# Mask first in the attention scores, last products by column halves, a last norm in pieces, and the reciprocal root on POOL

## The chip, the cores and the metric

The kernel runs on one core of a Trainium2 chip. The metric is the device time of one execution in microseconds (us); lower is better. The engines are TensorE (PE in the profile, its weight loads PEld), VectorE (DVE), ScalarE (ACT), GpSimd (POOL), and SyncE (SP), whose queue issues the weight DMAs.

## The reference

The kernel computes a small decoder trunk in float32: 256 tokens of width 1024, two layers, each a mixer and a channel mixer with a residual add around both, and a last norm.

```python
def rms_norm(x, g):
    y = x * lax.rsqrt(jnp.mean(x * x, axis=-1, keepdims=True) + 1e-6)
    return y * g

for i in range(2):
    h = rms_norm(x, attn_norm[i])
    if i == 0:
        x = x + even_mixer(h, ...)     # heads A: 8 of 64, one shared key, top-64 of indexer scores
                                       # heads B: 8 of 64, causal; one output projection for both
    else:
        x = x + mla_mixer(h, ...)      # 16 heads, scores over 64 + 32 columns, causal
    h = rms_norm(x, ffn_norm[i])
    x = x + peer_ffn(h, ...)           # 8 heads, 16 of 16384 experts each, by product keys
return rms_norm(x, final_norm)
```

In each attention the scores of a 128-row block of queries get a mask (causal, or for heads A the keys that the indexer selected), then softmax, then the weighted sum of the values.

## The kernel before, in words

x stays in SBUF as four tiles x[tb][j] of 128 tokens by 512 columns: tb is the token block, j the column half. The stages run one after the other in the span: the even mixer (0 to 148 us), the first expert layer `peer` (149 to 947), the MLA mixer (948 to 1068), the second expert layer (1070 to 1868), the last norm.

Float32 products are made from a high half `hi` and a low half `lo` of each operand (fp32r), three matmuls for one product (hi by hi, lo by hi, hi by lo). The class `Weights` streams the weights: SP loads `raw`, ACT makes `hi` (L69), DVE makes `lo` (L70), and `split(j)` does that some four units ahead of the one that PE uses. The pools of `hi` and `lo` have five buffers, so a new split waits until PE has done with an older unit.

The last four units of a layer's final product go through `last4` (L82), which hands out products for token block 0, then 1; after a block, `add_to_x` (L459) adds both of its column halves to x on DVE (L463). The next layer begins with transposes of x on PE (`to_T`, L288). The tile framework schedules the recorded operations, so the rows of an engine can stand in another order than the code; the adds are recorded at a high priority.

`attention` (L347) treats four heads at a time. For each query block qb it takes two PSUM banks with two heads in each; for each head it issues QK (L372) and then a product of the identity `identb` with a bf16 mask (L374), which adds the mask to the scores in PSUM. DVE takes the row maxima (L379), ACT the exponential (L383), PE transposes P (L397, L399) and multiplies it with the values (L413, L414). The heads of a group are named by their first: B8 is the group of heads 8 to 11 in the even mixer, A4 that of heads 4 to 7. An operand of an even-numbered head lies in partitions 0 to 63, of an odd one in partitions 64 to 127 (even mixer); in MLA it fills 96. Attention steps are interleaved with the projections by a plan (PLAN0, PLAN1); the last two groups of the even mixer, A0 and B12, run after the input projections, with the output projection behind them.

`rsqrt` (L248) makes 1/sqrt(mean + eps) on DVE, by a shifted integer guess and three Newton steps on one column at a time. It serves `x_rstd` (L270; square sums on ACT, four calls over both token blocks and two in the last norm) and the two inner norms of MLA. `finish` (L810) is the last norm: the gain times x on POOL (L819), the factor on ACT (L822) and DVE (L823), four stores from SP (L825).

## Time and profile before

| | us |
|---|---|
| median of 3 runs | 1882.4 (1880.84 to 1884.98) |
| the profiled execution's own time | 1880.96 |
| its span on the core | 1879.2 |
| PE busy | 1852.2 (99%) |
| DVE busy | 1447.2 (77%) |
| ACT busy | 1247.3 (66%) |
| POOL busy | 6.4 |

A busy matmul counts from its start to a modelled end, so PE at 99% says that PE nearly always has an instruction at work, not that each runs at its peak. The rows further down show starts and durations; a start of one PE instruction taken from the start of the next gives its real pace.

### The profile page before, as it was taken

How to read it: one execution, taken by the hardware profiler on the slowest of the kernel's cores; microseconds unless marked ns; L12 is line 12 of the kernel's file. 1: busy time of each engine (PE TensorE's matmuls, PEld its weight loads, DVE VectorE, ACT ScalarE, POOL GpSimd, SP SyncE). 2: the span in 40 equal slices, each digit the busy share in tenths (PEclk: the TensorE clock that was granted, in tenths of full speed). 3: DMA queues.
4: the chain of work that ended last, by engine and by line, in shares of the span. 5: the costliest groups of instructions: out<-in, count | busy, mean ns of one | idle time of the engine just before them, and what ended most of it. 6: DMA issues, size and time to landing. Idle time of an engine off the chain costs nothing.

```text
span 1879.2 us, 35739 instructions
## 1 busy us (share of the span) xinstructions
PE 1852.2 (99%) x12588; PEld 1664.2 (89%) x12588; DVE 1447.2 (77%) x3710; ACT 1247.3 (66%) x3060; POOL 6.4 (0%) x10
## 2 busy tenths in 40 slices
PE   8999999999999999999999999999999999999997
PEld 7769999999999888888888799999999988888886
DVE  7958998888898666666677699988888976666665
ACT  5646556888887555555576665688888865555554
POOL 0000000000000000000000000000000000000001
PEclk9989999999999999999999999999999999999999
DMA  6415565555555555556554345655555555555554
GB/s 191 134 46 170 163 197 182 168 169 174 165 170 179 191 193 193 191 193 192 188 162 136 122 139 190 190 174 165 172 167 169 171 189 191 192 192 193 192 193 136
DMA packets 90179, 323.33 MB, mean 172 GB/s; under 512 B 10512, under 2 KB 10896, under 8 KB 89744
## 3 DMA queue, kind: packets, MB, share of 16 engines
q1 hardware_dynamic: 88704, 318.71, 52.6%
q8 instruction: 99, 1.62, 0.3%
q0 software_dynamic: 288, 2.10, 0.3%
q14 instruction: 80, 0.66, 0.1%
q10 hardware_dynamic: 1008, 0.25, 0.1%
HBM read 319.97 MB, written 1.05 MB: 171 GB/s over the span
## 4 chain that ended last, share of the span: by engine, by line
PE 92%; DVE 6%; ACT 1%; issue 1%; DMA 0%; ACTq 0%; DVEq 0%
PE S L806 13%; PE S L807 13%; PE S L808 13%; PE acc L1079 12%; PE acc L1080 12%; PE acc L1078 12%; PE scp L990 3%; PE pj L301 2%; PE pj L303 2%; PE pj L302 2%; DVE lo L70 2%; PE bk L372 1%; DVE A L834 1%; DVE A L831 1%; DVE A L838 1%; PE pj L438 1%
## 5 line engine op out<-in xcount | busy, mean ns | idle before, releaser
L69 ACT ACTIVATE hi<-raw 128x512 fp32r<-128x512 f32 (+2 forms) x1214 | 756.0, 628 | 566.6 <-DVE lo L70 198.0
L70 DVE TENSOR_TENSOR lo<-raw,hi 128x512 fp32r<-128x512 f32 (+2 forms) x1214 | 826.2, 685 | 351.4 <-ACT hi L69 344.8
L806 PE MATMUL S<-hi,hi 128*128 128x256 f32 x2048 | 579.3, 283 | 1.8 <-ACT A L1019 1.8
L808 PE MATMUL S<-hi,lo 128*128 128x256 f32 x2048 | 568.9, 278 | 0.4
L807 PE MATMUL S<-lo,hi 128*128 128x256 f32 x2048 | 568.7, 278 | 0.0
L806 PEld LDWEIGHTS S<-hi,hi 128*128 128x128 f32 x2048 | 386.0, 188 | 2.6 <-ACT A L1019 2.6
L808 PEld LDWEIGHTS S<-hi,lo 128*128 128x128 f32 x2048 | 384.7, 188 | 1.2 <-DVE lo L70 1.1
L807 PEld LDWEIGHTS S<-lo,hi 128*128 128x128 f32 x2048 | 385.4, 188 | 0.0
L1079 PE MATMUL acc<-lo,ohB 128*128 128x512 f32 x512 | 201.2, 393 | 0.0
L1079 PE MATMUL acc<-lo,ohA 128*128 128x512 f32 x512 | 201.2, 393 | 0.0
L1080 PE MATMUL acc<-hi,ohA 128*128 128x512 f32 x512 | 199.9, 391 | 0.0
L1080 PE MATMUL acc<-hi,ohB 128*128 128x512 f32 x512 | 199.2, 391 | 0.0
L1078 PE MATMUL acc<-hi,ohA 128*128 128x512 f32 x512 | 159.2, 390 | 0.0
L1078 PE MATMUL acc<-hi,ohB 128*128 128x512 f32 x512 | 159.2, 390 | 0.0
L955 ACT ACTIVATE ohB<-ohB,RA 128x128 bf16<-128x128 bf16 x256 | 117.2, 525 | 0.0
L1078 PEld LDWEIGHTS acc<-hi,ohA 128*128 128x128 f32 x512 | 96.1, 188 | 22.0
L1078 PEld LDWEIGHTS acc<-hi,ohB 128*128 128x128 f32 x512 | 96.1, 188 | 21.9
L1079 PEld LDWEIGHTS acc<-lo,ohA 128*128 128x128 f32 x512 | 96.2, 188 | 20.8
L1079 PEld LDWEIGHTS acc<-lo,ohB 128*128 128x128 f32 x512 | 96.2, 188 | 20.7
L1080 PEld LDWEIGHTS acc<-hi,ohB 128*128 128x128 f32 x512 | 96.2, 188 | 20.3
L1080 PEld LDWEIGHTS acc<-hi,ohA 128*128 128x128 f32 x512 | 96.2, 188 | 20.3
L957 ACT ACTIVATE ohB<-iota,RA 128x128 bf16<-128x128 f32 x256 | 84.1, 435 | 0.0
(263 smaller groups left out, 2465.8 us busy)
## 6 DMA issues: line engine op xcount, KB each, us to landing
raw<-in_pu SPq DMA_DIRECT2D x256, 512.0 KB, 3.6
raw<-in_pv SPq DMA_DIRECT2D x256, 512.0 KB, 4.3
raw<-in_pq SPq DMA_DIRECT2D x32, 512.0 KB, 3.6
raw<-in_w SPq DMA_DIRECT2D x20, 512.0 KB, 3.7
raw<-in_uq SPq DMA_DIRECT2D x9, 512.0 KB, 4.0
raw<-in_w SPq DMA_DIRECT2D x12, 352.0 KB, 2.9
raw<-in_w0o SPq DMA_DIRECT2D x8, 512.0 KB, 3.6
raw<-in_w1o SPq DMA_DIRECT2D x8, 512.0 KB, 3.9
```

The lines of the kernel that those rows point to most:

```text
L69: self.nc.scalar.activation(hi[:, :w], src, AF.Copy)
L70: self.nc.vector.tensor_tensor(lo[:, :w], src, hi[:, :w].bitcast(F32), op=OP.subtract)
L301: nc.tensor.matmul(ps[tb], hi[c][:, t], a, start=st, stop=False)
L806: nc.tensor.matmul(p, a, hi[c], start=first and i == 0, stop=False)
L807: nc.tensor.matmul(p, a, lo[c], start=False, stop=False)
L808: nc.tensor.matmul(p, b, hi[c], start=False, stop=last and i == 3)
L955: nc.scalar.activation(e[:, j // 2, :, j % 2], e[:, j // 2, :, j % 2], AF.Relu, bias=r[1], scale=r[2])
L957: nc.scalar.activation(e[:, j // 2, :, j % 2], iota, AF.Square, bias=r[0], scale=-1.0)
L990: nc.tensor.matmul(p[:, i], E[:, 1, i // 2, :, i % 2], G[:, s, i // 2, :, i % 2], start=i + s == 0, stop=True, skip_group_check=True)
L1078: nc.tensor.matmul(o, a[:, 0, t], w[0], start=b == 0, stop=False)
L1079: nc.tensor.matmul(o, a[:, 0, t], w[1], start=False, stop=False)
L1080: nc.tensor.matmul(o, a[:, 1, t], w[0], start=False, stop=b == NK - 1)
```

## The change

It has five parts. In `attention`, one mask product over both heads of a bank comes first (it starts the accumulation), and the four QK follow in the order of the heads, which alternate between the two banks. `last4` goes through the column halves outside and the token blocks inside, and after each of the four pieces yields, so that a piece of x is added at a time; the new splits are asked for as token block 1 has used a unit. `rsqrt` adds, scales and takes the power -0.5 on POOL, with a [128, 16] float32 constant `mhalf` (64 bytes in each partition). The last norm takes its square sums piece by piece behind the adds, multiplies one column half by the gain on POOL and the other on DVE together with the factor, and sends two of the four stores from ACT's queue.

```diff
     def last4(self, products):
-        j = self.pos
+        k = self.pos
         w = [self.next(self.look - i) for i in range(4)]
-        for tb in range(2):
-            for i in range(4):
-                products(i, w[i], tb)
-                if tb == 1:
-                    self.split(j + self.look + 1 + i)
-            yield tb
+        for j in range(2):
+            for tb in range(2):
+                for i in (j, j + 2):
+                    products(i, w[i], tb)
+                    if tb == 1:
+                        k += 1
+                        self.split(k + self.look)
+                yield tb, j
...
+        mhalf = cp.tile([128, 16], F32, name="mhalf")
+        nc.gpsimd.memset(mhalf, -0.5)
         def rsqrt(parts, n, name):
             k = parts[0].shape[1]
             v = small.tile([128, k], F32, name=name + "v")
-            nc.vector.tensor_scalar(v, parts[0], 1.0 / n, EPS, op0=OP.mult, op1=OP.add)
+            s = parts[0]
             for p in parts[1:]:
-                nc.vector.scalar_tensor_tensor(v, p, 1.0 / n, v, op0=OP.mult, op1=OP.add)
+                nc.gpsimd.tensor_tensor(v, s, p, op=OP.add)
+                s = v
+            nc.gpsimd.tensor_scalar(v, s, 1.0 / n, EPS, op0=OP.mult, op1=OP.add)
             y = small.tile([128, k], F32, name=name + "y")
-            t = small.tile([128, k], F32, name=name + "t")
-            nc.vector.tensor_single_scalar(t.bitcast(U32), v.bitcast(U32), 1, op=OP.logical_shift_right)
...
-            for c in (3.0, 12.0, 768.0):
...
-            nc.vector.tensor_scalar(y, y, -1.0 / 8192, None, op0=OP.mult)
+            nc.gpsimd.tensor_tensor(y, v, mhalf[:, :1].to_broadcast([128, k]), op=OP.pow)
             return y
...
-                for i in (0, 2, 1, 3):
-                    h = hs[i]
-                    o = v[i % 2][:, i // 2]
-                    l, r = qk(h, qb, nk)
-                    nc.tensor.matmul(o, l, r, start=True, stop=False, skip_group_check=True)
-                    mk, k0 = masks(h, qb)
-                    nc.tensor.matmul(o[:, k0:], identb, mk, start=False, stop=True, skip_group_check=True)
+                mk, k0 = masks(hs[0], qb)
+                for a in range(2):
+                    nc.tensor.matmul(v[a][:, :, k0:], identb, mk[:, None, :].to_broadcast([128, 2, nk - k0]),
+                                     start=True, stop=False, skip_group_check=True)
+                for i in range(4):
+                    l, r = qk(hs[i], qb, nk)
+                    nc.tensor.matmul(v[i % 2][:, i // 2], l, r, start=False, stop=True, skip_group_check=True)
...
+                    def part(tb, j):
...
+                        nc.scalar.activation(ps2.tile([128, 512], F32, name="S"), x[tb][j], AF.Square,
+                                             accum_out=ssq[:, tb, j:j + 1])
+                        if j == 0:
+                            nc.gpsimd.tensor_tensor(y[:, h[0]], x[tb][0], g[:, h[0]], op=OP.mult)
+                            return
+                        r = rsqrt([ssq[:, tb, 0:1], ssq[:, tb, 1:2]], D, f"fin{tb}")
+                        nc.scalar.activation(y[:, h[0]], y[:, h[0]], AF.Copy, scale=r)
+                        nc.vector.scalar_tensor_tensor(y[:, h[1]], x[tb][1], r, g[:, h[1]], op0=OP.mult, op1=OP.mult)
+                        for i in range(2):
+                            (nc.sync, nc.scalar)[1 - i].dma_start(out[tb * 128:(tb + 1) * 128, h[i]], y[:, h[i]])
...
-                for tb in W.last4(lambda i, w, tb: mm(NK - 2 + i // 2, ws[i // 2], w, tb, i % 2)):
-                    add_to_x(tb, lambda j: acc[tb][j])
-                if final:
-                    finish()
+                last = finish() if final else None
+                for tb, j in W.last4(lambda i, w, tb: mm(NK - 2 + i // 2, ws[i // 2], w, tb, i % 2)):
+                    add_to_x(tb, j, acc[tb][j])
+                    if final:
+                        last(tb, j)
```

The lines of the changed kernel are numbered a little differently: QK stays L372, its mask becomes L368, the adds become L460, the transposes L285, and `rsqrt` spans L254 to L265.

How PE's rows stand at group B8, first query block, before (`bk` are the two banks, `kbT` and `qbT` the keys and queries, `cnegb` the causal mask):

```order
L372 MATMUL bk_943<-kbT0_116,qbT0_114 128x128
L374 LDWEIGHTS identb_95
L374 MATMUL bk_943<-cnegb_96,identb_95 128x128
L372 MATMUL bk_943<-kbT0_116,qbT0_114 128x128
L374 LDWEIGHTS identb_95
L374 MATMUL bk_943<-cnegb_96,identb_95 128x128
L372 MATMUL bk_944<-kbT0_116,qbT0_114 128x128
L374 LDWEIGHTS identb_95
L374 MATMUL bk_944<-cnegb_96,identb_95 128x128
L372 MATMUL bk_944<-kbT0_116,qbT0_114 128x128
L374 LDWEIGHTS identb_95
```

And with the change:

```order
L368 LDWEIGHTS identb_95
L368 MATMUL bk_930<-cnegb_96,identb_95 128x256
L368 LDWEIGHTS identb_95
L368 MATMUL bk_931<-cnegb_96,identb_95 128x256
L372 MATMUL bk_930<-kbT0_118,qbT0_116 128x128
L372 MATMUL bk_931<-kbT0_118,qbT0_116 128x128
L372 MATMUL bk_930<-kbT0_118,qbT0_116 128x128
L372 MATMUL bk_931<-kbT0_118,qbT0_116 128x128
```

Two masks of 256 columns stand ahead of four QK that go from bank to bank; before, a mask of 128 columns stood behind each QK.

PE's rows at the start of the last two attention groups of the even mixer (group A0, first query block, with the selection mask `selm0`), before:

```order
L372 MATMUL bk_1245<-kkT_118,qaT_112 128x128
L374 LDWEIGHTS identb_95
L374 MATMUL bk_1245<-selm0_138,identb_95 128x128
L372 MATMUL bk_1245<-kkT_118,qaT_112 128x128
L374 LDWEIGHTS identb_95
L374 MATMUL bk_1245<-selm0_138,identb_95 128x128
L372 MATMUL bk_1246<-kkT_118,qaT_112 128x128
```

And with the change:

```order
L368 LDWEIGHTS identb_95
L368 MATMUL bk_1224<-selm0_140,identb_95 128x256
L372 MATMUL bk_1224<-kkT_120,qaT_114 128x128 x2
L368 LDWEIGHTS identb_95
L368 MATMUL bk_1225<-selm0_140,identb_95 128x256
L372 MATMUL bk_1225<-kkT_120,qaT_114 128x128 x2
L368 LDWEIGHTS identb_95
L368 MATMUL bk_1244<-cnegb_96,identb_95 128x256
L372 MATMUL bk_1244<-kbT1_119,qbT1_117 128x128 x2
```

Here the scheduler puts each bank's mask directly ahead of that bank's two QK ("x2" are two QK in a row), and the next bank's mask behind them.

DVE's rows at the end of the first expert layer (x00 and x01 are token block 0, x10 and x11 token block 1; `lo` are low halves of weights of MLA), before:

```order
L70 TENSOR_TENSOR lo_12191<-raw_12133,hi_12190 128x352
L463 TENSOR_TENSOR x00_73<-x00_73,acc_9004 128x512
L463 TENSOR_TENSOR x10_75<-x10_75,acc_9006 128x512
L70 TENSOR_TENSOR lo_12198<-raw_12133,hi_12197 128x352
L463 TENSOR_TENSOR x01_74<-x01_74,acc_9005 128x512
L463 TENSOR_TENSOR x11_76<-x11_76,acc_9007 128x512
L70 TENSOR_TENSOR lo_12207<-raw_12158,hi_12206 128x352
```

And with the change:

```order
L70 TENSOR_TENSOR lo_12131<-raw_12064,hi_12130 128x352
L460 TENSOR_TENSOR x00_73<-x00_73,acc_8960 128x512
L70 TENSOR_TENSOR lo_12140<-raw_12089,hi_12139 128x352
L460 TENSOR_TENSOR x10_75<-x10_75,acc_8962 128x512
L70 TENSOR_TENSOR lo_12155<-raw_12089,hi_12154 128x352
L460 TENSOR_TENSOR x01_74<-x01_74,acc_8961 128x512
L460 TENSOR_TENSOR x11_76<-x11_76,acc_8963 128x512
L70 TENSOR_TENSOR lo_12164<-raw_12114,hi_12163 128x352
```

A low half now stands between the first add and the second, and another between the second and the third; before there was one, in the middle.

## Rows read from the trace of the kernel before

Times in rows are us from the start of the span.

**Rows 1.** The page's parts 1 and 2: busy us of each engine (share of the span, instructions), and the clock that TensorE was granted in 40 slices of the span, 47 us each, in tenths of full speed.

```profile
PE 1852.2 (99%) x12588; PEld 1664.2 (89%) x12588; DVE 1447.2 (77%) x3710; ACT 1247.3 (66%) x3060; POOL 6.4 (0%) x10
...
PEclk9989999999999999999999999999999999999999
```

**Rows 2.** The waits of PE over the whole span: what it waited for, us in total, times, longest.

```profile
PE scp L288 <- DVE x L463: 3.6, 2, 1.9
```

**Rows 3.** The timeline of PE at group B8, the first attention group of the even mixer (start us, duration us, engine, line, operation, shapes, how many): first QK, first mask and second QK of the first query block, first QK of the second block, and the product behind them.

```profile
72.10 0.48 PE L372 MATMUL bk<-kbT,qbT 64*128 64x128 f32 x2
72.52 0.23 PE L374 MATMUL bk<-cnegb,identb 128*128 128x128 bf16 x1
...
74.41 0.70 PE L372 MATMUL bk<-kbT,qbT 64*128 64x256 f32 x2
...
77.44 0.48 PE L301 MATMUL pj<-hi,hi 128*128 128x512 f32 x1
```

**Rows 4.** The timeline of PE at the index scores (L572), 128 columns at 44 us and 256 columns at 56 us, with the product behind each.

```profile
44.11 0.71 PE L572 MATMUL bk<-kkT,iqT 64*128 64x128 f32 x8
44.75 0.50 PE L301 MATMUL pj<-hi,hi 128*128 128x512 f32 x1
...
56.32 1.13 PE L572 MATMUL bk<-kkT,iqT 64*128 64x256 f32 x8
57.38 0.50 PE L301 MATMUL pj<-hi,hi 128*128 128x512 f32 x1
```

**Rows 5.** The timeline of PE at group A4, second query block: the first QK and the instruction behind it, then the stretch from its first mask to the product behind it.

```profile
91.99 0.70 PE L372 MATMUL bk<-kkT,qaT 64*128 64x256 f32 x2
92.62 0.65 PE L413 MATMUL bk<-pT,vb 128*64 128x256 f32 x2
...
94.85 0.28 PE L374 MATMUL bk<-selm,identb 128*128 128x256 bf16 x1
95.06 0.70 PE L372 MATMUL bk<-kkT,qaT 64*128 64x256 f32 x2
...
96.68 0.48 PE L438 MATMUL pj<-hi,oT 128*128 128x512 f32 x1
```

**Rows 6.** Busy time by stretches, the sum over 70 to 100 us.

```profile
sum 30.00, PE 30.00 PEld 20.30 DVE 26.07 ACT 17.32 POOL 0.00; mean PE 10.00 PEld 6.77 DVE 8.69 ACT 5.77 POOL 0.00
```

**Rows 7.** The timeline of PE from the first QK of the last two attention groups of the even mixer: the first instruction, a QK of the second query block with its mask, the first transpose of P, the first product of the output projection.

```profile
107.36 0.49 PE L372 MATMUL bk<-kkT,qaT 64*128 64x128 f32 x2
...
112.87 1.22 PE L372 MATMUL bk<-kbT,qbT 64*128 64x256 f32 x2
114.03 0.29 PE L374 MATMUL bk<-cnegb,identb 128*128 128x128 bf16 x1
...
122.75 0.64 PE L397 MATMUL bk<-ident,P 128*128 128x128 f32 x2
...
131.43 0.50 PE L438 MATMUL pj<-hi,oT 128*128 128x512 f32 x1
```

**Rows 8.** Busy time by stretches, two of the last attention stretch (us of PE, PEld, DVE, ACT, POOL with their instructions, then granted TensorE clock, DMA share, GB/s).

```profile
114.00:117.00 3.00, 3.00 (x9) 1.33 (x8) 0.82 (x3) 1.60 (x6) 0.00 (x0) 0.50 0.00 0
126.00:129.00 3.00, 3.00 (x22) 2.08 (x21) 1.43 (x3) 1.12 (x3) 0.00 (x0) 0.98 0.00 0
```

**Rows 9.** The timeline of PE at the first attention group of MLA: a mask, the next QK and the QK after that.

```profile
1008.35 0.22 PE L374 MATMUL bk<-cnegb,identb 128*128 128x128 bf16 x1
1008.40 0.44 PE L372 MATMUL bk<-kT,qT 96*128 96x128 f32 x2
...
1008.74 0.44 PE L372 MATMUL bk<-kT,qT 96*128 96x128 f32 x2
```

**Rows 10.** The timeline of all engines at the end of the first expert layer: the last product, the adds to x (L463), the low half of a weight (L70) between them, the first transposes of MLA.

```profile
947.02 0.40 PE L1080 MATMUL acc<-hi,ohA 128*128 128x512 f32 x1
947.10 0.52 DVE L70 TENSOR_TENSOR lo<-raw,hi 128x352 fp32r<-128x352 f32 x1
...
947.53 1.28 DVE L463 TENSOR_TENSOR x<-x,acc 128x512 f32<-128x512 f32 x2
...
948.87 0.66 PE L288 MATMUL bk<-ident,x 128*128 128x128 f32 x4 [1.45 <-DVE x L463]
```

**Rows 11.** The timeline of ACT in the first expert layer: the last read of a square sum, and the scaled x.

```profile
161.37 0.18 ACT L275 ACTIVATION_READ_ACCUMULATOR S<-x 128x1 f32 x1
...
165.44 0.71 ACT L796 ACTIVATE xn<-x,xn2y 128x512 f32<-128x512 f32 x1
```

**Rows 12.** The timeline of POOL: the last of its four constants, and its multiplies in the last norm.

```profile
0.34 0.10 POOL L1150 MEMSET const-uint8-127<- 128x1 uint8 x1
...
1867.22 4.98 POOL L819 TENSOR_TENSOR raw<-x,raw 128x512 f32<-128x512 f32 x4 [798.13 <-DVE x L463]
```

**Rows 13.** The timeline of all engines at the end of the kernel: the last two products, the last read of a square sum, the last two operations of DVE.

```profile
1867.57 0.39 PE L1079 MATMUL acc<-lo,ohA 128*128 128x512 f32 x1
...
1867.80 0.40 PE L1080 MATMUL acc<-hi,ohA 128*128 128x512 f32 x1
...
1869.74 0.19 ACT L275 ACTIVATION_READ_ACCUMULATOR S<-x 128x1 f32 x1
...
1874.21 0.15 DVE L267 TENSOR_SCALAR xn1y<-xn1y 128x1 f32<-128x1 f32 x1
1874.47 0.49 DVE L823 TENSOR_SCALAR raw<-raw,xn1y 128x512 f32<-128x512 f32 x1
```

## What the change should do to the time

> **What bounds the kernel now.** I read the page's busy shares first: PE is busy 1852.2 of 1879.2 us, DVE 1447.2, ACT 1247.3, POOL almost not at all [rows 1]. A microsecond is gained where PE gets shorter work, or where PE stands still. The PEclk line shows one more thing: nine tenths or more of full clock in every slice but the third, 94 to 141 us, which has an 8. Next come PE's waits: it stands still at the three boundaries between layers, where the first transposes of the next layer wait for an add to x, 3.6 us in two of them [rows 2] and 1.5 us in one [rows 10]. After the last matmul, at 1867.80, another 11 us pass [rows 13]. So four places can pay: the attention scores, the clock's hole, the boundaries, the tail. The two expert layers hold nearly all of the matmuls, and their inner loops are as before.
>
> **Mask first: even mixer, groups B8 and A4.** PE's rows for B8 show each head as a QK of two instructions from 72.10 and its mask at 72.52; four heads of the first query block take 72.10 to 74.41, 2.31 us, and four of the second 74.41 to 77.44, 3.03 us [rows 3]. The change puts two wide masks ahead and lets the four QK alternate between banks, and since heads 0 and 1 lie in partitions 0 to 63 and 64 to 127, between halves of the array. What alternating QK cost, the index scores show, which have the same shape (64x128, 64x256) and alternate already: eight instructions, four heads' worth, take 44.11 to 44.75 = 0.64 us, and with 256 columns 56.32 to 57.38 = 1.06 us [rows 4]. A mask of 256 columns is some 0.21 us (94.85 to the QK at 95.06, the instruction behind it on PE) [rows 5]. So the first block becomes 0.64 + 2 x 0.21 = 1.06, a gain of 1.25; the second 1.06 + 0.42 = 1.48, a gain of 1.55.
>
> That alternation is worth 0.42 to 0.16 us per head has a rule beside it. The Trainium skill, "TensorE: Matmul & The Clock Gate", Part 3, The mechanism, says that a weight load passes matmuls in flight only if its row group differs. By it the alternating blocks gain as above and blocks whose neighbouring QK share a row group gain nothing on the QK; by a sum that gave every block the index scores' price, the last stretch below would gain some 6 us at full clock and not 0.75. The rows agree with the rule as far as they go.
>
> For A4 the order has mask, QK, mask, QK, QK, QK in the first block. Four heads of 0.58 now (the pitch of rows 3) are 2.3; afterwards I count 2 x 0.21 for masks, 0.42 for each QK that stands against a mask and 0.16 for the rest, 1.6: gain 0.7. The second block is now 0.63 + 0.63 for two early QK (91.99 to 92.62 is one) and 1.83 from 94.85 to 96.68 [rows 5], 3.1 together; two masks of 512 columns (0.23 each, the pitch of a product of 512 columns, as at 1867.57 and 1867.80 [rows 13]) and 1.06 make 1.5: gain 1.55. It now needs its selection mask before its first QK; that mask is written some 4 us before PE comes to it, so no wait follows. Together PE loses 5.05 us of work. DVE, however, is busy 26.07 of the 30 us from 70 to 100 [rows 6], so it can give up only 3.9 us before it is the bound. I take **-4** (bounds -1.5, if the two engines alternate less well, and -5).
>
> **Mask first: the last two groups, 107.36 to 131.43.** The output projection at 131.43 ends a stretch in which PE has attention alone. At 107.36 a head takes 0.58; from 112.87 a head's 256-column QK takes 1.16, and the transposes of P begin at 122.75 [rows 7]. The granted clock is 0.50 from 114 to 117 and back at 0.98 from 126 to 129 [rows 8], that is, the engine falls to 1.2 GHz after some 5 us in which it had 64-row QK and masks alone, and has 2.4 GHz back some 3 us after the transposes begin. In the new order a bank gets mask, QK, QK here, both QK from the same half, so they keep 0.42 (0.69 with 256 columns), and only every second mask goes: eight of 0.1 to 0.16 us, less what the kept ones grow, about 0.75 us at full clock. If the fall comes as long after the stretch's start as now, what is saved ahead of it pulls other work to full clock, and what is saved behind it counts double: together **-1.5**. From above, +1: the clock could fall earlier. From below, -7: kept at 2.4 GHz, the 13 us until 126 shrink by some 6.
>
> **Mask first: MLA.** A head is 0.34 us (1008.40 to 1008.74), of which the mask is 0.05 (1008.35 to 1008.40) [rows 9]; QK of 96 rows fill both halves and gain nothing by alternating, and a mask over two heads streams the same columns. Sixteen heads twice: **-0.5** (0 to -1.6, all of the pitch).
>
> **Column halves at the boundaries.** One expects DVE to have a single add left when PE stops. Between the first expert layer and MLA it now does: lo at 947.10, two adds from 947.53, transposes at 948.87, 1.85 us after the last product's start at 947.02 [rows 10]. But the transposes' wait, in both programs, is for the count of the last of the four adds, so no transpose starts sooner on its own column. And of the four weight halves of the last step, the second one is now released six products before the end, not earlier, which puts its successor's split (ACT hi, then DVE lo) between the adds: the new order is x00, lo, x10, lo, x01, x11. By counting from the products they wait for (0.23 us apart, 0.4 from a product's start to its reader, an add 0.64, a lo 0.43 as at 947.10 to 947.53) x00 starts 1.4 us before the last product's start, and x11 1.4 after it; the transposes follow at about 2.05, 0.2 later than now. The same count gives no change for the other two, which have five operations in the row before and after. **0** in all (-0.7 if the adds get in front, +1 if lo runs late).
>
> **Reciprocal root on POOL, norms inside.** In the first expert layer the last square sum is read at 161.37 and the scaled x follows at 165.44, with Newton's 17 small DVE operations and three lo between [rows 11]. They go; three POOL operations come, and the scaled x stands two splits further forward in the queues of ACT and DVE, so that hi and lo queue behind it. Nothing prices a small POOL operation but the memset of 0.10 (128x1) and the multiply of 4.98 / 4 = 1.25 us (128x512) [rows 12]; at either price the chain, 0.3 to 3.8 us, is not longer than the present 4.1, and PE waits for no x norm now. **0**: the cover is the hi and lo halves made ahead (four of them, some 5 us of PE), gone if one operation takes over 2 us. The 64 bytes of the constant move later buffers by 64 bytes; no row speaks for a price, 0.
>
> **The last norm.** Now the last square sum is read at 1869.74 and the last scaling, at 1874.47, ends 4.24 us before the span does [rows 13]. Of the 4.7 us between, the Newton chain is nearly all, behind which ACT and DVE scale. Two of the four stores now leave from ACT's queue, behind its scalings. After: five POOL operations stand behind that read (one add, two scalings, two roots), then ACT or DVE scale once (0.7). With p per operation the last scaling ends at 1869.9 + 5p + 0.7 (+ 0.5 for handing from engine to engine), now 1874.96; p = 0.10 gives -3.4, p = 1.25 gives +2.4. The shape is the memset's, 128x1, but two inputs are read and a power taken: p = 0.3, **-2.4**. The skill's "GPSIMD Engine Reference" calls POOL's elementwise work about half as fast as DVE's; the rows agree (1.25 [rows 12] against 0.64 of an add on DVE [rows 10]), and twice DVE's small operation of 0.15 [rows 13] would give the same -2.4.
>
> **Sum.** -4 - 1.5 - 0.5 + 0 + 0 - 2.4 = -8.4 on the profiled execution's 1880.96: 1872.6. The median of the runs is 1.4 above that execution; I say **1873**.
>
> **Rivals.** (a) The clock holds through the last attention stretch, because it is shorter: -5.5 more, 1867.5. For it: the 5.3 us of B8 keep full clock. Against: the QK there stay in pairs and take over 10 us in a row. 0.15. (b) DVE bounds the even mixer, or POOL's operation costs 0.8: half of a gain, -4, 1877.5. For it DVE's 26.07 of 30. 0.17. (c) Alternation doesn't do it: a wide mask is a full-height load between half-height QK, and no row has that sequence; saved masks turn into waits for the row maxima on DVE. Tail alone, -2.4 or less: 1879.5. 0.11. (d) Slower: POOL's root is a long operation. At p = 2.0 the tail alone costs 5 x 1.7 = 8.5 more than I take, and the whole sum is gone; beyond, each x norm's 3p outlasts the 6 us that the queues hold ready, and hi and lo behind the scaled x on ACT and DVE stall PE. At p = 3, +5 and two stalls of 3 us, 1892. Against: a multiply of 512 columns takes 1.25. 0.05. (e) The clock falls in B8 or MLA too: +5, 1886. 0.02. My own forecast has 0.50.
>
> Two in a thousand, 3.8 us, is what a measurement of this kernel can tell. Faster by that: my case, (a), most of (b): 0.80; within: the rest of (b), (c): 0.13; slower 0.07. The range from 1866 to 1880.5 holds all but (d), (e), the end of (a) and a piece of (c).
>
> **What would show it.** B8's four QK from first mask to next product near 1.1 and 1.5 us, A4's second near 1.5; in the last stretch PEclk 0.50 again for 12 us or more and pairs of QK at 0.42 a head before; the waits of the transposes for x within 0.3 us of now; POOL's operations of 128x1 near 0.3 us and the last read of a square sum to the span's end near 7. I am wrong if the last stretch has no half clock, if DVE idles nowhere from 70 to 100 while PE waits, or if POOL's roots are microseconds long.

## The result, and the profile after

The changed kernel takes 1897.91 us (1897.23 to 1898.49) against 1882.38 of the kernel before in the same comparison: a ratio of 1.0081, 95% interval 1.0063 to 1.0098. Forecast were 1873 us and a range up to 1880.5; it is slower by 15.5 us, and outside.

The page of the changed kernel, busy times and the slices of its granted clock (rows of before: [rows 1]):

```profile
PE 1870.7 (99%) x12556; PEld 1671.6 (88%) x12556; DVE 1432.1 (76%) x3586; ACT 1244.5 (66%) x3060; POOL 14.5 (1%) x33
...
PEclk9999999999999999999999999999999999999999
```

PE has 32 instructions fewer and is busy 18.5 us longer. The 8 in the clock's third slice is gone. So the engine got more of its clock and less work, and still needs longer. Cutting the span at the first transposes of each layer and at the last product shows where (us, worked out from the starts in the traces; the third kernel, the changed one with 128 unread bytes, is met below):

| stretch | before | after | after, less before | changed kernel + 128 bytes |
|---|---|---|---|---|
| even mixer (to the transposes) | 149.76 | 138.89 | -10.9 | 137.38 |
| first expert layer | 799.11 | 813.93 | +14.8 | 799.14 |
| MLA | 121.23 | 121.49 | +0.3 | 120.73 |
| second expert layer | 797.70 | 812.49 | +14.8 | 797.15 |
| last product to the end | 11.38 | 9.40 | -2.0 | 9.42 |

The stretches that the change rewrites become shorter. The two expert layers, whose inner loops it does not touch, lose 29.6 us. Busy time by stretches in the first expert layer (columns as in [rows 8]; 200 to 500 is the half with products of 256 columns, 600 to 800 the one with 512), before:

```profile
200.00:500.00 300.00, 299.35 (x2736) 296.93 (x2736) 267.69 (x797) 227.06 (x626) 0.00 (x0) 1.00 0.55 176
600.00:800.00 200.00, 200.00 (x875) 164.11 (x874) 125.01 (x220) 114.60 (x219) 0.00 (x0) 1.00 0.59 192
```

And after:

```profile
200.00:500.00 300.00, 299.63 (x2694) 297.07 (x2693) 262.41 (x753) 225.95 (x629) 0.00 (x0) 1.00 0.55 174
600.00:800.00 200.00, 200.00 (x859) 160.29 (x858) 123.21 (x216) 111.70 (x214) 0.00 (x0) 1.00 0.59 189
```

PE never stands still in 600 to 800, the clock is 1.00 in both, and 859 products fit where 875 did: 232.8 ns each against 228.6. All other engines and the DMA have room, as before. So neither a wait nor the clock nor another engine's load does it: each product itself takes longer. The rows of single products show it as well; before, then after, the timeline of PE from 700 us:

```profile
700.51 0.39 PE L1079 MATMUL acc<-lo,ohB 128*128 128x512 f32 x1
700.74 0.39 PE L1080 MATMUL acc<-hi,ohB 128*128 128x512 f32 x1
700.97 0.39 PE L1079 MATMUL acc<-lo,ohB 128*128 128x512 f32 x1
701.20 0.39 PE L1080 MATMUL acc<-hi,ohB 128*128 128x512 f32 x1
```

```profile
700.25 0.39 PE L1085 MATMUL acc<-hi,ohB 128*128 128x512 f32 x1
700.48 0.63 PE L1083 MATMUL acc<-hi,ohB 128*128 128x512 f32 x2
700.95 0.39 PE L1084 MATMUL acc<-lo,ohB 128*128 128x512 f32 x1
```

The duration column says 0.39 in both and hides the difference; the pace stands in the starts (700.51 to 701.20 is three products in 0.69; 700.25 to 700.95 three in 0.70; over a whole stretch the mean is 228.9 and 233.3 ns). Products of 256 columns go from a mean of about 114.9 ns to 117.8. With 3072 of these and 1536 of 512 columns in a layer that is 3072 x 2.9 + 1536 x 4.4 ns = 15.7 us, for 14.8 measured.

### The profile page after: what moved, and what is told of

Same layout as the page of the kernel before. It is cut to its first block, busy times and chain, and to the rows that moved or that the text cites. A ratio compares the mean times of both kernels' runs of the same rounds, so it can differ in the third digit from the quotient of the medians.

```text
span 1896.2 us, 35560 instructions
## 1 busy us (share of the span) xinstructions
PE 1870.7 (99%) x12556; PEld 1671.6 (88%) x12556; DVE 1432.1 (76%) x3586; ACT 1244.5 (66%) x3060; POOL 14.5 (1%) x33
## 4 chain that ended last, share of the span: by engine, by line
PE 94%; DVE 4%; ACT 1%; issue 1%; DMA 0%; DVEq 0%; POOLq 0%; POOL 0%; ACTq 0%
PE S L803 14%; PE S L804 14%; PE S L805 14%; PE acc L1083 13%; PE acc L1084 13%; PE acc L1085 13%; PE scp L995 3%; PE pj L298 2%; PE pj L300 2%; PE pj L299 2%; DVE lo L70 1%; PE bk L372 1%; PE scp L1032 1%; PE pj L436 1%; PE pj L437 1%; PE pj L438 1%
## 5 line engine op out<-in xcount | busy, mean ns | idle before, releaser
L70 DVE TENSOR_TENSOR lo<-raw,hi 128x512 fp32r<-128x512 f32 (+2 forms) x1214 | 825.7, 685 | 386.9 <-ACT hi L69 380.2
```

The costliest lines, as they stand in the source:

```text
L70: self.nc.vector.tensor_tensor(lo[:, :w], src, hi[:, :w].bitcast(F32), op=OP.subtract)
```

## The experiments

### Is it the constant, or the address of the block behind it?

The constant moves all later buffers by 64 bytes in each partition. Three kernels change its size alone, to 32, 96 and 128 bytes in the changed kernel; the fourth adds 64 unread bytes to the kernel before.

```diff
# c32, c96, c128: the changed kernel with 8, 24, 32 columns
-        mhalf = cp.tile([128, 16], F32, name="mhalf")
+        mhalf = cp.tile([128, 32], F32, name="mhalf")
# b64: the kernel before
+        pad = cp.tile([128, 16], F32, name="pad")
+        nc.gpsimd.memset(pad, -0.5)
```

> The changed kernel with its constant at 128 bytes instead of 64 (mhalf [128, 32] for [128, 16]); nothing else. All buffers behind it move by 64 bytes, so each starts at the same place within 128 bytes as in the kernel before. Address theory: the expert layers go back to a pitch of 0.2285 us for products of 512 columns (now 0.2333) and 0.114 for 256 (now 0.118), some 800 us a layer less 2 (now 814), so about 1897.9 - 30 = 1868 us. Rival, POOL's new work or the new order slows TensorE: the pitch stays 0.2333, about 1898 us.

> The kernel before with a constant of 64 bytes added (filled once, read by nobody); nothing else. Address theory: both expert layers take 814 us instead of 798, in all about 1882.4 + 30 = 1912 us, and the pitch is 0.2333. Rival, POOL's new work or the new order: unchanged, 1882 us.

> The changed kernel with a constant of 32 bytes: the weights' hi and lo start at 0 within 128 bytes (32 in the changed kernel, 96 in the one before). Address theory says that the place matters but not which is best: if a start on a multiple of 64 is as good as 96 or better, 1868 us or less; if only 96 is good, 1898. Rival (POOL's work): 1898 us.

> The changed kernel with a constant of 96 bytes: the weights' hi and lo start at 64 within 128 bytes. Address theory: like the 32-byte constant if a multiple of 64 is what counts (1868 or less both), different from it if the half of a 128-byte block counts. Rival (POOL's work): 1898 us.

Measured: c128 1897.53 us (ratio to before 1.0084, 1.0067 to 1.0101), c32 1898.72 (1.009, 1.0073 to 1.0107), c96 1898.3 (1.0089, 1.0072 to 1.0106), b64 1881.8 (0.9998, 0.9989 to 1.0008). The place of the block of all later buffers plays no part, and the constant is innocent. My first theory fell here.

### Which part of the change brings it?

mask is the kernel before with the new attention order alone; pool with the root on POOL alone, constant included; last4 with the column halves alone; nopool is the changed kernel with the Newton steps on DVE and no constant.

> The kernel before with mask-first attention alone. The place of the buffers is out as a cause, so it is one of the parts that slows the products. If POOL's new operations do it: the products keep 0.229 us, the even mixer ends near 139 us as in the changed kernel, in all 1882.4 - 11 = 1871 us. If the new attention does it (TensorE's pace hangs on what it did earlier): 0.233 us from the start of the first expert layer on, 1882.4 - 11 + 30 = 1901.

> The kernel before with the reciprocal root on POOL alone (constant of 64 bytes included, last norm as before but by the new root). If POOL's operations slow TensorE: pitch 0.233 us behind the first of them at about 16 us, 1882.4 + 30 - 2 = 1910 us. If the attention does it: pitch 0.229 and about 1880 us (the last norm gains 2).

> The kernel before with the last products by column halves alone (the last norm as before). The prediction's count: the three boundaries within 0.3 us of before and the time the same, 1882.4 us. If this part slows the products: 1912 us.

> The changed kernel with the reciprocal root back on DVE (Newton steps, no constant); attention, column halves and last norm as changed. If POOL's operations slow TensorE: pitch 0.229, 1897.9 - 30 + 2 = 1870 us. If the attention or the column halves do: pitch 0.233, about 1900 us.

Measured: mask 1869.23 (0.9926, 0.9909 to 0.9942), pool 1882.93 (1.0, 0.999 to 1.0009), last4 1881.32 (0.999, 0.9981 to 1.0), nopool 1905.11 (1.0117, 1.01 to 1.0134). Products of 512 columns run at 228.9 ns in the first three and at 232.4 in nopool. None of these three parts alone slows the expert layers, and taking the POOL root out of the whole makes it worse. What the slow kernels share is not an instruction. The programs' buffer addresses show what differs: a small pool lies between the buffers of the weights and those of the stages. It loses the temporaries of the Newton steps and gains the tiles of the new last norm, in the changed kernel 128 bytes less in all. So the stage buffers stand at another distance from the weight buffers: the start address of the x operand in the first half of the expert layers, less that of the weights' first `hi`, is 132544 bytes before and 132416 after; modulo 256 (what is left beyond whole 256s) that is 192 and 64. The pieces of the last norm, the part that was not run alone, are in two kernels of the next section that run at 228.9 ns (gap128, nopool_gap64).

The pool kernel teaches a second thing. Its tail, last product to end, is 11.46 us, no shorter than 11.38 before. The timeline of POOL there shows why:

```profile
1868.65 4.96 POOL L813 TENSOR_TENSOR raw<-x,raw 128x512 f32<-128x512 f32 x4 [784.45 <-DVE x L457]
...
1873.57 0.34 POOL L257 TENSOR_TENSOR xn1v<-ssq 128x1 f32<-128x1 f32 x2
...
1874.53 1.10 POOL L261 TENSOR_TENSOR xn1y<-xn1v,mhalf 128x1 f32<-128x1 f32 x2
```

The root queues behind POOL's four multiplies. In nopool, with the pieces but without POOL's root, the tail is 9.81; with both it is 9.40. The last norm's gain is mostly the pieces' (-1.6 us); the root takes off another 0.4.

### Is it the distance?

Unread bytes in the small pool move the stage buffers against the weight buffers and change no instruction that PE, ACT or DVE runs. The pool holds each tile twice, so 16 float32 columns are 128 bytes there.

```diff
# gap128: the changed kernel; b_gap128, b_gap64: the kernel before with 16, 8 columns; nopool_gap64: nopool with 8
+        gap = small.tile([128, 16], F32, name="gap")
+        nc.gpsimd.memset(gap, 0.0)
```

> The changed kernel with 128 bytes that nobody reads, put between the weights' hi and lo and the buffers of the stages behind them. Distance theory: what counts is how far a product's two operands in SBUF lie from each other; in every kernel so far whose products run at 0.229 us the expert layers' operands are 192 bytes apart beyond whole 256s, in the changed kernel and its three relatives 64, in the one with DVE roots 128. Here it is 192 again: pitch 0.229, about 1868 us. Rival, the pieces of the last norm (the one part not run without the slow pace): unchanged, 1898.

> The kernel before with the same 128 unread bytes at the same place, nothing else. Distance theory: the expert layers' operands lie 64 beyond whole 256s as in the changed kernel; pitch 0.2333 and 0.118, 1882.4 + 30 = 1912 us. Rival, the last norm's pieces: 1882 us.

> The kernel before with 64 unread bytes there: the distance is 0 beyond whole 256s in the expert layers, a value that no kernel had. Distance theory: another pace than 0.229 is likely, and 0 may be the best or the worst of the four, from 1875 to 1920 us. Rival, the last norm's pieces: 1882.

> The changed kernel with roots on DVE (1905 us, distance 128) and 64 unread bytes there, which makes the distance 192. Distance theory: pitch 0.229 again, about 1870 us; beside the first of this set it also tells what POOL's root is worth. Rival, the last norm's pieces: 1905.

Measured: **gap128 1866.13 us (0.9912, 0.9895 to 0.9928)**, the fastest of this study; b_gap128 1915.05 (1.0174, 1.0157 to 1.0191); b_gap64 1909.32 (1.014, 1.0123 to 1.0157); nopool_gap64 1867.53 (0.9921, 0.9904 to 0.9937). 128 bytes that nobody reads take 31.8 us off the changed kernel, and put 32.2 on the kernel before (1882.87 in that comparison). nopool_gap64 beside gap128 puts POOL's root, in the whole change, at 1.4 us, which their overlapping intervals do not tell from nothing. b_gap64 in the two stretches of the first expert layer (700 to 800 here, since its products of 512 columns begin later):

```profile
200.00:500.00 300.00, 299.77 (x2641) 297.80 (x2640) 260.17 (x788) 219.50 (x591) 0.00 (x0) 1.00 0.53 169
...
700.00:800.00 100.00, 100.00 (x443) 82.84 (x442) 63.07 (x111) 58.18 (x111) 0.00 (x0) 1.00 0.61 192
```

One half is slower than after (2641 instructions for 2694), the other faster than before (443 in 100 us for 438 in that stretch of the kernel before). The two halves have different distances that are best for them. Each pace below is the mean difference between consecutive starts of such products in the expert layers:

| distance to the weights, modulo 256 | 512 columns | 256 columns | kernels |
|---|---|---|---|
| 0 | 226.7 ns | 119.9 ns | b_gap64 |
| 192 | 228.9 | 114.9 | before, b64, mask, mask_pairs, pool, last4, gap128, nopool_gap64 |
| 128 | 232.4 | 119.3 | nopool |
| 64 | 233.3 | 117.8 | after, c32, c96, c128, b_gap128 |

No kernel of these rows falls out of its row, whatever else it changes, and whole multiples of 256 (pool stands 256 bytes nearer than before) do nothing. The Trainium skill, "TensorE: Matmul & The Clock Gate", Part 2, Step-by-step: what each phase is for, gives PE two read ports, one for the streamed operand and one for weight loads, so that a load takes nothing from a running product; nothing in it lets the distance matter. Here it does, by up to 2.9% of a product of 512 columns and 4.4% of one of 256. The runs show that two addresses count relative to each other; they do not show what collides.

The 114.9 ns are a mean of two paces. At distance 192 the products of 256 columns run now at one and now at the other: in the kernel before at 113.5 ns from 380 to 480 us and at 117.8 from 500 to 520, at clock 1.00 in both. At distance 64 nearly all run at the slower one. What makes the pace change within a run is not shown.

### Which operands, and is there a still better layout?

In the first half PE loads the streamed weights and x passes through; in the second half it loads the one-hot tiles `ohA` and `ohB`, and the streamed weights pass through. v0 is gap128 with 64 bytes more ahead of the one-hot tiles and 192 behind them: the second half should have distance 0, the first keep 192. u224 and u160 move the x operands of the first half as well, to 224 and 160. v0_pa and pa64 move the buffer A1 of the activations, back to its place in v0 and out of it in gap128.

```diff
# v0: gap128 and
+                hp.tile([128, 16], F32, name="gap2")
+                rawpool.tile([128, 48], F32, name="gap3")
# v0_pa: v0 and 192 bytes ahead of A1; pa64: gap128 and 64 bytes ahead of A1
+                pa.tile([128, 48], F32, name="gap4")
```

> The changed kernel with the 128 unread bytes (1866 us), and in the expert layers 64 more ahead of the one-hot weights of the second half and 192 behind them, so that only the distance of the second half's operands changes: 0 beyond whole 256s, where it was 192. If the pace of a product is set by the distance of its own two operands: 226.7 ns in the second half (as the kernel before with 64 bytes had there), the first half's 256-column products as they were, 3072 x 2.2 ns = 6.8 us less, 1859.3 us. Rival, one layout of the whole SBUF sets the pace of everything: both halves move, or neither (1866).

> As the one before, with the first half's x operands moved by 32 bytes (224 beyond whole 256s from the weights, where 192 gave 113.3 to 115 ns and 0 gave 119.9). If the pace goes smoothly with the distance: between, 116 to 118 ns, +10 to +25 us on 1859. If it goes in blocks of 64 bytes, as 192 or as 0: 1859 or 1895. The second half stays at 226.7.

> As the one before, moved to the other side: 160 beyond whole 256s, between 192 (113.3 to 115 ns) and 128 (119.2). Smoothly: 115 to 118 ns, 1865 to 1885 us; in blocks of 64: 1859 or 1890. A pace under 113.3 would be a better place than any so far.

> Kernel v0 with 192 unread bytes more at the start of the pool of the activations, so that the activations' buffer A1 stands again at its place of the kernel before, modulo 256, while the one-hot tiles keep the distance 0 from the streamed weights. If A1's place is what slowed the products of 256 columns in v0 (a mean of some 117 ns where the kernel before has 114.9), they go back to some 114.9 and the products of 512 columns stay at 226.7: about 1859 us. If the place of the one-hot tiles or of the rows' indices did it, the time stays at v0's 1873.

> Kernel gap128 with 64 unread bytes ahead of the activations' buffer A1 alone. If A1's place slows the products of 256 columns, they go from 114.9 to some 117 ns and the time from 1866 to 1873 to 1880 us; the products of 512 columns stay at 228.9. If A1's place plays no part, the time stays at 1866.

Measured: v0 1873.43 (0.9955, 0.9939 to 0.9972), u224 1878.65 (0.998, 0.997 to 0.9989), u160 1880.9 (0.9994, 0.9984 to 1.0003), v0_pa 1873.69 (0.9947, 0.993 to 0.9964), pa64 1866.58 (0.9909, 0.9893 to 0.9926). The second half runs at 226.7 ns in all of v0, u224, u160 and v0_pa, so its pace follows the distance of the one-hot tiles from the weights. But in v0 the first half slowed too, to a mean of 117 ns, with its own operands where they were, and took back more than the gain (1859.3 us were expected). The first half at 224 and 160 has 118.3 and 118.9 ns; beside v0, from which these two differ in the place of the first half's operands (and whole multiples of 256), both neighbours of 192 are slower. v0 in the second half:

```profile
600.00:800.00 200.00, 200.00 (x884) 165.69 (x883) 126.97 (x222) 115.50 (x222) 0.00 (x0) 1.00 0.61 194
```

884 instructions for 875. In the first half, the products of 256 columns alone (PE busy us and their number, then clock, DMA share, GB/s), gap128:

```profile
200.00:300.00 100.00, 99.40 (x842) 1.00 0.61 190
320.00:560.00 240.00, 224.33 (x1838) 1.00 0.53 168
```

And v0:

```profile
200.00:300.00 100.00, 99.22 (x839) 1.00 0.61 190
320.00:560.00 240.00, 224.65 (x1797) 1.00 0.52 165
```

From 200 to 300 us the two do nearly the same work; the loss is all in the later stretch, from 310 us on, in which PE also multiplies one-hot tiles with each other. There four fifths of gap128's products run at the faster of the two paces (mean 114.3 ns), and one in sixteen of v0's (117.5). A1 is not the reason: v0_pa puts it back and stays at 117 ns, pa64 moves it and stays at 114.9. Of the tiles that v0_pa leaves at another distance, PE reads `act` in the first expert layer up to 197 us only, so the place of the one-hot tiles is what is left. Why it slows products that do not read them remains open, and a layout with both halves at their best was not found.

### Do the QK gain by alternating between the halves?

mask_pairs is mask with the four heads in the order 0, 2, 1, 3, so that QK that share a half of the array stand next to each other.

```diff
-                for i in range(4):
+                for i in (0, 2, 1, 3):
```

> Mask-first attention alone (1869.2 us), but its QK in the order of the heads 0, 2, 1, 3, so that two QK from the same half of the partitions follow each other everywhere, as they already do in the last stretch. If alternating halves is what makes QK cheap in the early groups: two QK take 0.64 us there as in the last stretch, not 0.32, B8's blocks take 1.7 and 2.5 us instead of 1.0 and 1.4, A4's second 2.5 instead of 1.5; +2 to +3 us, about 1871.7, and the clock of the last stretch holds, since that stretch is as it was. Rival, the clock holds there only because the early groups are shorter: half clock again, +6 more, 1878.

Measured: 1868.74 (0.9922, 0.9905 to 0.9939), the same as mask. The timeline of PE, B8:

```profile
72.21 0.39 PE L371 MATMUL bk<-cnegb,identb 128*128 128x256 bf16 x2
72.53 0.72 PE L375 MATMUL bk<-kbT,qbT 64*128 64x128 f32 x8
73.18 0.39 PE L371 MATMUL bk<-cnegb,identb 128*128 128x256 bf16 x2
...
88.12 0.39 PE L371 MATMUL bk<-selm,identb 128*128 128x512 bf16 x1
88.44 1.13 PE L375 MATMUL bk<-kkT,qaT 64*128 64x256 f32 x4
89.50 0.39 PE L371 MATMUL bk<-selm,identb 128*128 128x512 bf16 x1
89.82 1.13 PE L375 MATMUL bk<-kkT,qaT 64*128 64x256 f32 x4
```

Eight QK instructions take 0.65 us (72.53 to 73.18) in pairs as well as in turns. In A4 (88.12 on), where a mask over the full height stands between the two halves' QK, the block takes 2.8 us (88.12 to the next product at 90.94) and not the 1.7 of gap128: four instructions of one half take 1.06 us, as long as eight of both halves [rows 4]. So it isn't alternation that makes QK cheap but that nothing of full height stands between the QK of the two halves; the prediction's "blocks whose neighbouring QK share a row group gain nothing on the QK" does not hold here. The extra 1 us of A4 costs no time: from 70 to 100 us DVE is busy 28.62 us in this kernel as in gap128, and PE only stands idle for less (0.4 us for 1.9). Nor is the change's own order in B8 what keeps the clock up later: here too the last attention stretch is at 1.00.

## Why the prediction was wrong, point by point

**The layout: the step that failed.** "The 64 bytes of the constant move later buffers by 64 bytes; no row speaks for a price, 0", and "their inner loops are as before". The 64 bytes did cost nothing (b64). But I looked at the one new buffer that the change names, and not at the buffers that it takes away and adds in the small pool; and I took it that a loop with unchanged instructions keeps its time. The term was +29.6 us in the expert layers, and some 2.3 in the two mixers (after less gap128: 1.5 and 0.8; in the even mixer, whose own distance went from 0 to 128, products of 512 columns go from 227 to 230 ns before to 232 to 233.5). With the distance put back the same instructions take 1866.13: 16.7 us less than the kernel before in the same comparison (1882.87), at the lower end of the range, and next to the 1867.5 of rival (a). So without the layout the forecast of 1873 would still have been 7 us off; that part is the last attention stretch, below.

**Attention, B8, A4: right.** PE in the changed kernel at B8, then at A4's second block:

```profile
72.77 0.40 PE L368 MATMUL bk<-cnegb,identb 128*128 128x256 bf16 x2
73.10 0.71 PE L372 MATMUL bk<-kbT,qbT 64*128 64x128 f32 x8
73.75 0.39 PE L368 MATMUL bk<-cnegb,identb 128*128 128x256 bf16 x2
74.07 1.13 PE L372 MATMUL bk<-kbT,qbT 64*128 64x256 f32 x8
75.13 0.50 PE L298 MATMUL pj<-hi,hi 128*128 128x512 f32 x1
...
89.50 0.60 PE L368 MATMUL bk<-selm,identb 128*128 128x512 bf16 x2 [0.67 <-DVE selm L592]
90.03 1.14 PE L372 MATMUL bk<-kkT,qaT 64*128 64x256 f32 x8
91.22 0.66 PE L411 MATMUL bk<-pT,vb 128*64 128x256 f32 x4
```

B8's blocks take 0.98 and 1.38 us (forecast 1.06 and 1.48; [rows 3] had 2.31 and 3.03), A4's second 1.72 (1.5). The mask of A4 does come to be waited for, 0.67 us, against "no wait follows". As forecast, DVE becomes the bound (the three stretches of [rows 6]):

```profile
70.00:80.00 10.00, 10.00 (x54) 7.18 (x52) 9.97 (x34) 9.30 (x27) 0.00 (x0) 1.00 0.47 154
80.00:90.00 10.00, 9.33 (x55) 6.91 (x53) 10.00 (x30) 6.01 (x19) 0.00 (x0) 1.00 0.35 105
90.00:100.00 10.00, 9.29 (x53) 6.79 (x52) 8.66 (x18) 4.87 (x14) 0.00 (x0) 1.00 0.33 91
```

DVE is busy 28.63 of 30 us and PE stands idle for 1.4; in the two long pauses, 88.83 to 89.50 and 92.10 to 92.76, DVE is busy throughout. At unchanged distances (gap128) the last stretch begins at 102.50 and not at 107.36: -4.9 for a forecast of -4, bound -5. Of that, 0.7 us lie ahead of B8, which begins at 71.40 for 72.10 (70.73 in last4, whose code up to there is that of before); from B8 on it is 31.10 us for 35.26, -4.2.

**The last attention stretch: the rival's course, and my term mis-sized.** I took -1.5, with half clock again; rival (a), the clock held, had 0.15. It came true. The changed kernel by stretches:

```profile
104.00:108.00 4.00, 4.00 (x23) 2.98 (x24) 2.26 (x8) 3.35 (x16) 0.00 (x0) 1.00 0.00 0
108.00:112.00 4.00, 4.00 (x16) 2.26 (x16) 2.95 (x9) 3.54 (x16) 0.00 (x0) 1.00 0.00 0
112.00:116.00 4.00, 3.80 (x27) 2.50 (x25) 3.90 (x10) 2.63 (x10) 0.00 (x0) 1.00 0.00 0
```

Before, the engine was at 0.50 from 114 to 117 [rows 8]. Now the stretch takes 16.52 us (103.67 to 120.19; 102.50 to 119.02 in gap128) for 24.07 in [rows 7]: -7.55. Its QK were mis-sized too:

```profile
103.67 0.27 PE L368 MATMUL bk<-selm,identb 128*128 128x256 bf16 x1
103.87 0.71 PE L372 MATMUL bk<-kkT,qaT 64*128 64x128 f32 x4
104.51 0.28 PE L368 MATMUL bk<-selm,identb 128*128 128x256 bf16 x1
```

0.64 us for two heads is 0.32 a head, where I kept 0.42 of the old order: a mask behind every QK had cost 0.1 per head beyond its own time. So the part ahead of the transposes of P, 107.36 to 122.75 before, is over in 8.7 us (103.67 to 112.38), and the clock falls nowhere in it. All four kernels with the new order that were read there (after, gap128, mask, mask_pairs) hold 1.00; last4 and pool, with the old order, fall to 0.50 as the kernel before does. Rival (a) gave the shorter stretch as its reason; that does not come out of the traces, for before the clock fell 5.1 us after the stretch's start (1.00 from 107.4 to 112.4, 0.50 from 112.5 on), and the 8.7 us are longer than that. Why the new order keeps the clock up is open. The old order can lose it at B8 too, where the profiled execution of before did not: the clock is 0.50 from 76 to 79 us in last4 and from 75 to 81 in b64, and for 3 us or more there in pool, b_gap64 and b_gap128. No profile with the new order shows that, which may be why the medians of gap128 and before lie further apart (16.7 us) than the two profiled spans (15.4).

**MLA: right.** -0.5 forecast; 121.23 to 120.73 at unchanged distance.

**Boundaries: right, by the right count.** The transposes' waits for x are 3.5 and 1.6 us after (3.6 [rows 2] and 1.5 before). At the end of the first expert layer, the last product and DVE of the changed kernel:

```profile
950.85 0.40 PE L1085 MATMUL acc<-hi,ohA 128*128 128x512 f32 x1
951.06 0.52 DVE L70 TENSOR_TENSOR lo<-raw,hi 128x352 fp32r<-128x352 f32 x1
...
951.49 1.28 DVE L460 TENSOR_TENSOR x<-x,acc 128x512 f32<-128x512 f32 x2
...
952.82 0.44 PE L285 MATMUL bk<-ident,x 128*128 128x128 f32 x2 [1.58 <-DVE x L460]
```

A `lo` and the two last adds still stand behind the last product, and the transposes follow 1.97 us after its start, for 1.85 in [rows 10] and 2.05 forecast. last4 alone leaves the time as it was (1881.32, ratio 0.999, 0.9981 to 1.0).

**Reciprocal root: right.** Timeline of POOL in the first expert layer, and of ACT:

```profile
150.89 0.18 POOL L260 TENSOR_TENSOR xn2v<-ssq 128x2 f32<-128x2 f32 x1 [12.58 <-ACT S L272]
...
151.44 1.19 POOL L264 TENSOR_TENSOR xn2y<-xn2v,mhalf 128x2 f32<-128x2 f32 x1
```

```profile
150.61 0.18 ACT L272 ACTIVATION_READ_ACCUMULATOR S<-x 128x1 f32 x1
...
152.67 0.72 ACT L793 ACTIVATE xn<-x,xn2y 128x512 f32<-128x512 f32 x1 [1.08 <-POOL xn2y L264]
```

2.1 us from the last read to the scaled x for 4.1 in [rows 11], inside the 0.3 to 3.8 given, and worth nothing, since nobody waited for it (pool alone 1882.93, ratio 1.0).

**The last norm: nearly right.** The last product starts at 1886.80; then the changed kernel shows:

```profile
1888.70 0.18 ACT L819 ACTIVATION_READ_ACCUMULATOR S<-x 128x1 f32 x1
1888.96 0.19 POOL L260 TENSOR_TENSOR fin1v<-fssq 128x1 f32<-128x1 f32 x1
...
1889.78 0.55 POOL L264 TENSOR_TENSOR fin0y<-fin0v,mhalf 128x1 f32<-128x1 f32 x1
1890.30 0.55 POOL L264 TENSOR_TENSOR fin1y<-fin1v,mhalf 128x1 f32<-128x1 f32 x1
...
1891.03 0.75 DVE L826 SCALAR_TENSOR_TENSOR raw<-x,fin1y,raw 128x512 f32<-128x512 f32 x1
```

Add and scaling are 0.19 us, a root 0.55; the starts from 1888.96 to 1890.30 are 0.27 to 0.52 apart, for the p of 0.3 taken. From that read to the end 7.5 us (near 7 forecast), before 9.44: -1.9, and -2.0 from the last product on, for -2.4.

**The sum.** -4.9 - 7.55 - 0.5 - 2.0 = -15 at unchanged distance, and gap128's span is 15.4 shorter than before's; then +32.4 for the distances gives the +17.0 of the two profiled spans. Of the signs I had named for being wrong two came, the last stretch without half clock, which made the kernel faster, and DVE idle nowhere while PE waits from 70 to 100, which left that gain as it was (-4.2 for -4); the cause of the loss lay beside them all, in the layout. The prediction's own addition is off too: 1872.6 for the profiled execution and 1.4 more for the median are 1874.0, not 1873.

## What to carry to other kernels

An edit that takes away or adds a small buffer moves all that is allocated behind it, so print the buffer addresses of both kernels and compare the distances between the operands of the hot loop before believing that an untouched loop keeps its time. Read the pace of its products from their starts, in a stretch where PE has no idle time, in both profiles; where it differs at the same clock, put the distance back with unread bytes before you judge the edit itself. This change, judged as it stood, would have been thrown away with its 16 us; and where a gain in PE's work seems small, ask whether it also keeps the clock up.

## What the runs showed of the hardware that was not expected

- The pace of fp32r products at full clock depends on the distance between their two operands in SBUF modulo 256 bytes: 226.7 to 233.3 ns with 512 columns, a mean of 114.9 to 119.9 with 256, and the best of the distances tried is not the same for the two (0 and 192). With 256 columns it is not the distance alone: at 192 one run has stretches at 113.5 and at 117.8 ns, and with the one-hot tiles moved (v0) the mean is 117. The fp16 products of 128 columns keep 59 ns in both kernels.
- Where QK of the two half-height row groups stand together, eight instructions take 0.65 us, in either order; with a full-height mask between the groups, four take the time of eight (1.06 us with 256 columns).
- On POOL an add or scaling of one or two columns takes 0.18 to 0.20 us (one of 0.67), the power 0.55 us for one column and 0.69 to 1.19 for two; the first of the span, at 17.1 us, is no longer than the rest.
